# Grouped-query attention: keys written with every head twice, one more weight buffer, scores of two heads between the last query products

## The chip, the cores and the metric

The kernel runs on one core of a Trainium2 chip. The metric is device time of one execution in microseconds (us), the median over runs. The core has TensorE (matrix products; PE in the profile, and PEld for its weight loads), VectorE (DVE), ScalarE (ACT), GpSimd (POOL) and SyncE (SP), which only starts transfers. Each engine works through its own instructions in a fixed order and waits for others by semaphores.

## The reference

One inference step of a two-layer transformer trunk, D = 1024, for 512 latent tokens and 128 context (prompt) tokens. Layer 0 uses neighbourhood attention, layer 1 grouped-query attention with 16 query heads and 4 key heads of width 64. Only layer 1's attention bears on the change:

```python
q, k, v = jnp.split(h @ w_qkv, [1024, 1280], axis=-1)
q = rmsnorm(q.reshape(b, t, 16, 64), q_norm)      # per head
k = rmsnorm(k.reshape(b, t, 4, 64), k_norm)
...
qs = axial_rope(qs); ks_ = axial_rope(ks_)        # latent tokens alone
k_all = jnp.concatenate([ks_, cache_gqa_k[:, i]], axis=1)   # 512 + 128 cached keys
v_all = jnp.concatenate([vs, cache_gqa_v[:, i]], axis=1)
os_ = blocked_attention(qs, k_all, v_all)         # softmax(q k / 8) v, 4 query heads per key head
op = blocked_attention(qp, kp, vp)                # prompt tokens among themselves
```

Behind it come the output product, a residual with adaLN gates, and a gated ConvFFN. The new keys and values of the prompt are outputs too.

## The kernel before

All products run as three passes of split float32 (`hi`, `lo`): each operand is copied to a rounded high part (`wh`, `hT[0]`, `kh`) and a subtraction leaves the low part (`wl`, `hT[1]`, `kl`). The stage of the change lies between layer 0's feed-forward (which ends at about 852 us of the span) and layer 1's output product.

- **Token tiles.** The 640 tokens are five tiles `t` of 128: four latent, and the prompt (`t` = 4). The stage makes 15 product tiles, each a PSUM bank of 128 x 512 by 24 matmuls (`products`, tile name `gp`): first keys and values for `t` = 0 to 4 (`kv_tile`), then the first eight query heads for `t` = 4, 0, 1, 2, 3 (`q_tile`, `hq` = 0), then the other eight for `t` = 0 to 4 (`hq` = 1). Below they are numbered 0 to 14 in that order.
- **Per tile.** `head_rms` squares on ScalarE (`sq`), sums on VectorE (`ssh`), and takes the root on GpSimd (`vh`, `rh`). `head_norm` multiplies by it (`y`) and rotates: cosine product, four sine products into `sq` (VectorE), and their sum on GpSimd (into `kt` or `qt`). The rotation's tables `tab` are made once from `rot` and the gains `gn`, which small transfers on ScalarE's queue bring. Then TensorE transposes the tile into another bank (`turn_k`, `turn_q`, tiles `tk` and `tq`), and copies and subtractions write the high and low parts: `gkh`, `gkl` for keys, each head on both halves of the partitions, `gq` for queries.
- **Weights.** `gqa_w` loads a quarter of a 1024 x 512 group into `wr`, ScalarE copies it into `wh`, VectorE subtracts into `wl`. `wp` has four buffers of each. Those of the next group are split between the products of the last tile of a group (`ahead_of`), as each buffer's last reader is done.
- **Order.** TensorE's order is the order in which the program writes its instructions (`pe`, line 107). `step` holds back the norms by one tile and the transposes by `keep` tiles more, which the list `KP` sets to two for the first four key tiles and one for all others. On the other engines a scheduler orders the instructions by a model of its own.
- **PSUM.** `Banks` (line 74) is a queue: a tile takes the first free bank and is put behind the others when its last reader has been written. `bk.first` prefers one of two pools of four banks (`psx`, `psy`); `bk.drop(4)` takes `psy` out, when it is to be used for scores.
- **Prompt attention** of each key head is three items (`gqa_prompt`: scores, transpose, values) that `PSTEP` deals out behind given query tiles.
- **Units.** Then come 32 units, each a head and half of the latent tokens: scores of two token tiles into a double bank each (`s2`), minimum on VectorE (`nmg`), exponential on ScalarE (`gp`), scaling on GpSimd, transposes (`tp`, `pk`), values (`po`). `GORDER` lists the steps; the scores of a unit are made two units ahead. The scores of units 0 and 1 are written ahead of the first step, behind all query products.

Of the kernel before, what the change touches and what calls it, by code (L numbers as in the profile page):

```python
# [57 lines left out]
PSTEP = (3, 5, 6, 6, 8, 9)  # L58
WU = 29
TP = 1  # L60
PSN = 4
# [4 lines left out]
KP = (2, 2, 2, 2, 1)  # L66
# [35 lines left out]
def hybrid_step(ctx: ExitStack, tc: tile.TileContext, A, O):  # L102
# [1278 lines left out]
    def gqa_w(c0, u, low=None):  # L1381
        return wsplit(rows(wqkv, 2 * u, 2, c0, 512), 2, 512, low)
# [20 lines left out]
    rot = ap.tile([P, 2, 4, HD], F32, name="rot", bufs=1)  # L1403
    nc.scalar.dma_start(rot, A["k_rope"])
# [9 lines left out]
    tab = ap.tile([P, 2, 2, 4, HD], F32, name="tab", bufs=1)  # L1414
    for i in range(2):
        for j in range(2):
            nc.vector.tensor_mul(tab[:, i, j], rot[:, j], gn[:, i, j].unsqueeze(1).broadcast_to([P, 4, HD]))
# [3 lines left out]
    def head_rms(src, n):  # L1421

        sq = ap.tile([P, 8, HD], F32, tag="sq", name="sq")[:, 0:n, :]
        nc.scalar.activation(sq, src, AF.Square)
        ss = sm.tile([P, 8], F32, name="ssh")[:, 0:n]
        nc.vector.tensor_reduce(ss, sq, axis=AX.X, op=ALU.add)
        v = sm.tile([P, 8], F32, name="vh")[:, 0:n]
        nc.gpsimd.tensor_scalar(v, ss, 1.0 / HD, EPS, op0=ALU.mult, op1=ALU.add)
        r = sm.tile([P, 8], F32, name="rh")[:, 0:n]
        last_rms[0] = nc.gpsimd.tensor_tensor(r, v, mhalf.broadcast_to([P, n]), op=ALU.pow)  # L1430
        return sq, r

    def head_norm(dst, src, sq, r, t, i, n):

        y = ap.tile([P, 8, HD], F32, tag="y", name="y")[:, 0:n, :]
        nc.vector.tensor_mul(y, src, r.unsqueeze(2).broadcast_to([P, n, HD]))
        if t == 4:
            nc.vector.tensor_mul(dst, y, gn[:, i, 0].unsqueeze(1).broadcast_to([P, n, HD]))
            return
        nc.vector.tensor_mul(dst, y, tab[:, i, 0, t].unsqueeze(1).broadcast_to([P, n, HD]))  # L1440
# [3 lines left out]
        for b in range(2):  # L1444
            for a in range(2):
                nc.vector.tensor_mul(
                    s5[:, :, a, b, :], y5[:, :, a, 1 - b, :],
                    b4[:, a, b, :].unsqueeze(1).broadcast_to([P, n, 16]),
                )
        nc.gpsimd.tensor_add(dst, dst, sq)  # L1450

    def put_v(c, src):
        nc.scalar.copy(vt[:, c], src.rearrange("p (a d) -> p a d", a=4))

    def turn_k(src, cols):

        tp = bk.get("tk")
        for j in range(2):
            turn(tp[:, j * P : j * P + P], src[:, j * P : j * P + P], ident)
        tv = tp[:, 0:256].rearrange("p (a b) -> p a b", a=2)  # L1460
        for b in range(2):
            own, oth = own_oth(b)
            for part in (own, oth):
                nc.scalar.copy(kh[part, b::2, cols], tv[own])
            for part in (own, oth):
                nc.vector.tensor_sub(kl[part, b::2, cols], tv[own], f32(kh[own, b::2, cols]))
        bk.put(tp)

    def turn_q(src, hq, t):
# [5 lines left out]
        for b in range(2):  # L1475
            own, oth = own_oth(b)
            q = qst[hq][b]
            nc.scalar.copy(q[own, :, cs], tv[own])
            nc.vector.tensor_sub(q[oth, :, cs], tv[own], f32(q[own, :, cs]))
# [18 lines left out]
    def kv_tile(t, ws, *how):  # L1498

        ps = products(t, ws, *how)  # L1500
        st = head_rms(heads(ps[:, 0:256]), 4)
        put_v(t, ps[:, 256:512])
        if t == 4:
            vo = ap.tile([P, 256], F32, tag="kt", name="gvo", bufs=3)
            nc.scalar.copy(vo, ps[:, 256:512])
            nc.scalar.dma_start(O["new_gqa_v"][0, 0].rearrange("t h d -> t (h d)"), vo)

        def norm():
            kt = ap.tile([P, 256], F32, tag="kt", name="kt", bufs=3)
            head_norm(heads(kt), heads(ps[:, 0:256]), *st, t, 1, 4)  # L1510
            if t == 4:
                nc.scalar.dma_start(O["new_gqa_k"][0, 0].rearrange("t h d -> t (h d)"), kt)
            bk.put(ps)
            return lambda: turn_k(kt, slice(t * P, t * P + P) if t < 4 else slice(T, T + P))

        return norm

    def q_tile(t, hq, ws, *how):
        ps = products(t, ws, *how)
        st = head_rms(heads(ps), 8)  # L1520

        def norm():
            if hq and t == 4:
                qt = wp.tile([P, 512], F32, tag="wr", name="qt")
            else:
                qt = ap.tile([P, 512], F32, tag="qt", name="qt", bufs=3)
            head_norm(heads(qt), heads(ps), *st, t, 0, 8)
            bk.put(ps)
            return lambda: turn_q(qt, hq, t)

        return norm
# [29 lines left out]
    ck = ap.tile([P, 256], F32, tag="ck", name="ck", bufs=1)  # L1561
    nc.scalar.dma_start(ck, A["cache_gqa_k"][0, 0].rearrange("t h d -> t (h d)"))
    cv = ap.tile([P, 256], F32, tag="cv", name="cv", bufs=1)
    nc.scalar.dma_start(cv, A["cache_gqa_v"][0, 0].rearrange("t h d -> t (h d)"))
    norms, turns = deque(), deque()

    def step(tile=None, keep=1):
        if tile:
            norms.append(tile)
        while len(norms) > (1 if tile else 0):  # L1570
            turns.append(norms.popleft()())
            if tile:
                break
        while len(turns) > (keep if tile else 1):
            turns.popleft()()

    wqs = [[], []]

    def ahead_of(hq):
        return lambda u: wqs[hq].append(gqa_w(512 * hq, u))  # L1580

    for t in range(NT):
        step(kv_tile(t, wkv, t == 0, ahead_of(0) if t == 4 else None), KP[t])
        if t == 0:
            late[0]()
        elif t == 1:
            late[1]()
            xmp.close()
            pp_s = ExitStack()
            cur = [pp_s.enter_context(pool("prp", 1))]  # L1590
    turns.append(lambda: turn_k(ck, slice(NS, T)))
    put_v(5, cv)
    extra = deque()
    for hq in range(2):
        for n, t in enumerate(((4, 0, 1, 2, 3), (0, 1, 2, 3, 4))[hq]):
            if hq and n == PSN:
                bk.first = psx
            step(q_tile(t, hq, wqs[hq], n == 0, ahead_of(1) if 5 * hq + n == 4 else None))
            i = 5 * hq + n
            if n == 2:  # L1600
                extra.extend(gqa_prompt(2 * hq) + gqa_prompt(2 * hq + 1))
            for _ in range(PSTEP.count(i)):
                extra.popleft()()
    step()
    extra.extendleft(turns)
    pp_s.close()
    hp2.close()
    gqs.close()
    l_o1 = ExitStack()
    op1 = l_o1.enter_context(pool("o1"))  # L1610
    osp1 = [[op1.tile([P, T], F32R, name=f"p{i}{p}") for i in "hl"] for p in range(KC)]
    bk.first = None
    bk.drop(4)
    psy.close()
    with ExitStack() as s:
        ap = s.enter_context(pool("ga", 2, "right"))
        cur = [ap]
        sps = ExitStack()
        sps_p = sps.enter_context(pool("pss", space=PSUM))
        m1 = Mix(1, A["gqa_w_o"][0], lambda p, t: tuple(x[:, t * P : t * P + P] for x in osp1[p]))  # L1620
        ta = {}

        class Unit:


            def __init__(self, u):
                self.b, self.hf, self.p = u % 2, u // 2 % 2, u // 4
                self.h = 2 * self.p + self.b
# [193 lines left out]
```

## Time and profile before

| | us |
|---|---|
| median of three runs (lowest, highest) | 1609.09 (1608.65, 1611.68) |
| the profiled execution | 1610.03 |
| its span in the profile | 1608.2 |
| TensorE busy | 1541.6 (96%) |
| VectorE busy | 1023.0 (64%) |
| ScalarE busy | 860.6 (54%) |
| GpSimd busy | 722.2 (45%) |

The mean granted clock of TensorE was 0.983. A row of the timeline gives the start in us from the span's start, the duration in us, the engine, the line, the operation, what is written `<-` what is read, the shape, how often, and in square brackets the idle time of the engine before it with what ended it. A row of the waits gives who waited for whom: the total in us, how often, the longest. A row of the windows gives a stretch, its length, the busy time and count of PE, PEld, DVE, ACT and POOL, then the granted clock, the share of the transfer engines and GB/s. Line 114 is the helper through which all products go, line 117 that of all transposes, so the tile names tell them apart.

### The profile page before, as it was taken

To read this page: it belongs to the slowest core of one execution; us is meant where nothing else is said; L and a number is where in the kernel's file an instruction comes from. 1 tells how busy PE (TensorE), PEld (TensorE's weight loads), DVE (VectorE), ACT (ScalarE), POOL (GpSimd) and SP (SyncE) were. 2 spreads that over 40 slices of the span, in tenths; PEclk is the share of its full clock that TensorE was granted. 3 is DMA by queue.
4 is the path that set the end of the run, shared out by engine and by line. 5 is a ranking of instruction groups with operands and counts; after the bars stand their busy time and mean duration, and the time that the engine had idled before them with its cause. 6 is when DMAs were issued, how large, how long until landed. Compare 5 with 4: busy or idle time off the path is not lost.

```text
span 1608.2 us, 26065 instructions
## 1 busy us (share of the span) xinstructions
PE 1541.6 (96%) x9709; PEld 1360.4 (85%) x9709; DVE 1023.0 (64%) x1646; ACT 860.6 (54%) x1641; POOL 722.2 (45%) x613
## 2 busy tenths in 40 slices
PE   5999999899999999999999888999999999999998
PEld 3989899777999999988887666778899999998886
DVE  3453533538877666674656867774887888876554
ACT  3474655545565555554453536764555556565343
POOL 1554554324355445544443344441524565553433
PEclk8999999999999999999999998999999999999999
DMA  9745454236456566578573110004634333348664
GB/s 290 185 113 146 117 151 119 62 105 198 144 185 194 199 209 186 193 241 299 170 236 131 60 40 14 2 1 143 211 109 156 105 117 115 104 149 276 206 211 140
DMA packets 193211, 242.42 MB, mean 151 GB/s; under 512 B 11100, under 2 KB 149564, under 8 KB 193084
## 3 DMA queue, kind: packets, MB, share of 16 engines
q1 hardware_dynamic: 182224, 233.13, 45.4%
q10 hardware_dynamic: 10860, 7.62, 2.7%
q8 instruction: 76, 1.25, 0.3%
q14 instruction: 51, 0.42, 0.1%
HBM read 214.38 MB, written 26.34 MB: 150 GB/s over the span
## 4 chain that ended last, share of the span: by engine, by line
PE 73%; DVE 10%; POOL 6%; issue 4%; ACT 4%; DMA 2%; SPq 1%; ACTq 0%; POOLq 0%; DVEq 0%
PE acc L114 18%; PE ux L114 15%; PE y L114 7%; PE uz L114 6%; PE qk L114 5%; PE uy L114 4%; PE po L114 4%; PE s L114 4%; PE vp L114 3%; PE tp L117 3%; PE ada L114 2%; POOL wl L1112 1%; DVE al L1112 1%; POOL vl L1112 1%; DMA wf<-in_ada_w 1%
## 5 line engine op out<-in xcount | busy, mean ns | idle before, releaser
L167 POOL TENSOR_TENSOR wl<-wr,wh 128x1024 fp32r<-128x1024 f32 x74 | 181.5, 2455 | 263.4 <-ACT wh L165 255.2
L1112 POOL TENSOR_TENSOR wl<-wr,wh 128x1024 fp32r<-128x1024 f32 x80 | 194.2, 2448 | 46.1 <-ACT wh L1111 42.6
L114 PE MATMUL ux<-B,wh 128*128 128x322 f32 x832 | 201.9, 314 | 1.4 <-ACT u L1165 0.9
L1188 DVE SCALAR_TENSOR_TENSOR t<-C,cw,t 128x644 f32<-128x644 f32 x176 | 156.3, 888 | 49.1 <-ACT t L1186 48.4
L114 PE MATMUL acc<-wh,alo 128*128 128x512 f32 x440 | 172.3, 392 | 0.6 <-DVE alo L1081 0.6
L114 PE MATMUL acc<-wh,ahi 128*128 128x512 f32 x440 | 171.9, 391 | 0.0
L114 PE MATMUL acc<-wl,ahi 128*128 128x512 f32 x440 | 171.9, 391 | 0.0
L165 ACT CAST wh<-wr 128x1024 fp32r<-128x1024 f32 x140 | 145.5, 1048 | 33.5 <-DMA wr<-in_ffn_w_down 24.3
L114 PE MATMUL uz<-B,wh 128*128 128x322 f32 x640 | 156.5, 313 | 0.7 <-ACT v L1165 0.7
L114 PEld LDWEIGHTS ux<-B,wh 128*128 128x128 f32 x832 | 145.0, 190 | 4.3 <-ACT u L1165 1.2
L1081 DVE TENSOR_TENSOR alo<-ain,ahi 128x384 fp32r<-128x384 f32 (+1 forms) x88 | 77.3, 893 | 89.8 <-ACT ahi L1079 88.8
L114 PE MATMUL ux<-B,wl 128*128 128x322 f32 x416 | 130.1, 313 | 0.2
L114 PE MATMUL qk<-hT,wh 128*128 128x384 f32 (+1 forms) x512 | 122.8, 317 | 0.1
L114 PEld LDWEIGHTS uz<-B,wh 128*128 128x128 f32 x640 | 110.9, 188 | 3.6 <-ACT vh L1111 1.6
L1112 POOL TENSOR_TENSOR vl<-wr,vh 128x1024 fp32r<-128x1024 f32 x38 | 97.1, 2556 | 30.9 <-ACT vh L1111 30.5
L1111 ACT CAST wh<-wr 128x1024 fp32r<-128x1024 f32 x88 | 88.7, 1048 | 32.6 <-DVE wr L1135 31.4
L1186 ACT ACTIVATE t<-C,cw 128x644 f32<-128x644 f32 x88 | 78.6, 893 | 45.9 <-DVE C L1216 43.9
L114 PE MATMUL uz<-B,wl 128*128 128x322 f32 x320 | 99.5, 311 | 0.1
L167 DVE TENSOR_TENSOR wl<-wr,wh 128x1024 fp32r<-128x1024 f32 x66 | 84.5, 1293 | 23.6 <-ACT wh L165 23.1
L114 PEld LDWEIGHTS acc<-wh,alo 128*128 128x128 f32 x440 | 82.5, 188 | 19.1 <-DVE alo L1081 1.4
L1079 ACT CAST ahi<-ain 128x384 fp32r<-128x384 f32 (+1 forms) x88 | 40.1, 460 | 108.4 <-PE acc L114 91.4
L114 PEld LDWEIGHTS acc<-wl,ahi 128*128 128x128 f32 x440 | 82.6, 188 | 17.8
(249 smaller groups left out, 4010.2 us busy)
## 6 DMA issues: line engine op xcount, KB each, us to landing
wr<-in_ffn_w_up SPq DMA_DIRECT2D x88, 512.0 KB
wr<-in_ffn_w_down SPq DMA_DIRECT2D x88, 512.0 KB
wr<-in_ada_w SPq DMA_DIRECT2D x80, 512.0 KB
act<-act SPq DMA_DIRECT2D x44, 321.0 KB
wr<-in_na_w_qkv SPq DMA_DIRECT2D x24, 512.0 KB
mod<-modrow SPq DMA_DIRECT2D x20, 512.0 KB
ain<-act SPq DMA_DIRECT2D x44, 192.0 KB
wf<-in_ada_w SPq DMA_DIRECT2D x16, 512.0 KB
```

The source lines that it names most:

```text
L114: pe(nc.tensor.matmul(*a, **k))
L117: pe(nc.tensor.transpose(*a, **k))
L165: i = nc.scalar.copy(hi, raw)
L167: j = (low or nc.vector).tensor_sub(lo, raw, f32(hi))
L1079: pin(nc.scalar.copy(hi[:, 0 : c1 - c0], ain[:, 0 : c1 - c0]))
L1081: pin(nc.vector.tensor_sub(lo[:, 0 : c1 - c0], ain[:, 0 : c1 - c0], f32(hi[:, 0 : c1 - c0])))
L1111: nc.scalar.copy(hl[0], src)
L1112: low.tensor_sub(hl[1], src, f32(hl[0]))
L1186: nc.scalar.activation(t, taps(0), AF.Identity, bias=cw[:, 3, n : n + 1], scale=cw[:, 1, n : n + 1])
L1188: nc.vector.scalar_tensor_tensor(t, taps(d), cw[:, w, n : n + 1], t, op0=ALU.mult, op1=ALU.add)
```

## The change

- Keys are normed into a tile that holds every head twice, side by side (`kd`): the last addition writes both, or for the prompt two multiplications do. `turn_k` then makes four transposes instead of two and one copy and one subtraction over 128 partitions instead of four and four over 64. The cached keys are loaded twice into the same shape; the cached values go straight into `vt`.
- A pool `wx` holds one more `wh` and `wl`. Of each group one weight is split some tiles ahead, two during the last tile of the group before, and one behind it; two of the four subtractions go to GpSimd.
- `Prep` takes the place of `kv_tile`, `q_tile` and `step`. Of each tile the square sums are written within the next tile's products, its transposes behind the products two tiles on and ahead of the norm of the tile between. The table `KP` is gone.
- `bk.first` prefers `psx` from tile 10 on (before: tile 14), and `psy` is dropped at tile 12, where the scores' pool takes its place. The scores of units 0 and 1 are written within the products of tiles 12, 13 and 14 (`ESC`: tile and quarter, unit and half); their probabilities lie in four `wr` buffers. The last query tile is turned ahead of unit 2's step.
- `PSTEP` (now counted over all 15 tiles) puts the prompt's items behind tiles 8, 9, 10, 10, 11, 12; before it was, in that count, 8, 10, 11, 11, 13, 14.
- `pk` has five buffers of 512 instead of six. `rot` is gone: the table is loaded into `tab` and multiplied there. `o` returns its argument.

```diff
-PSTEP = (3, 5, 6, 6, 8, 9)
+PSTEP = (8, 9, 10, 10, 11, 12)
+ESC = {(12, 2): (0, 0), (13, 1): (0, 1), (13, 3): (1, 0), (14, 2): (1, 1)}
-PSN = 4
-KP = (2, 2, 2, 2, 1)
...
+    wx = gqs.enter_context(pool("wx", 1, "right"))
+    tab = ap.tile([P, 2, 2, 4, HD], F32, name="tab", bufs=1)
+    nc.scalar.dma_start(tab[:, 1], A["k_rope"])
...
+        if twice is not None:
+            dst, sq = (x.unsqueeze(2).broadcast_to([P, n, 2, HD]) for x in (dst, sq))
+        o(nc.gpsimd.tensor_add(dst if twice is None else twice, dst, sq))
...
     def turn_k(src, cols):
 
         tp = bk.get("tk")
-        for j in range(2):
-            turn(tp[:, j * P : j * P + P], src[:, j * P : j * P + P], ident)
-        tv = tp[:, 0:256].rearrange("p (a b) -> p a b", a=2)
-        for b in range(2):
-            own, oth = own_oth(b)
-            for part in (own, oth):
-                nc.scalar.copy(kh[part, b::2, cols], tv[own])
-            for part in (own, oth):
-                nc.vector.tensor_sub(kl[part, b::2, cols], tv[own], f32(kh[own, b::2, cols]))
+        for g in range(4):
+            turn(tp[:, g * P : g * P + P], src[:, g].rearrange("p a b -> p (a b)"), ident)
+        tv = tp.rearrange("p (a b) -> p a b", a=4)
+        o(nc.scalar.copy(kh[:, :, cols], tv))
+        o(nc.vector.tensor_sub(kl[:, :, cols], tv, f32(kh[:, :, cols])))
         bk.put(tp)
...
+    ck = ap.tile([P, 4, 2, HD], F32, name="ck", bufs=1)
+    for b in range(2):
+        nc.scalar.dma_start(ck[:, :, b, :], A["cache_gqa_k"][0, 0])
+    nc.scalar.dma_start(vt[:, 5], A["cache_gqa_v"][0, 0])
...
+    tiles = [Prep(None, t) for t in range(NT)]
+    tiles += [Prep(hq, t) for hq in range(2) for t in ((4, 0, 1, 2, 3), (0, 1, 2, 3, 4))[hq]]
+    group = [wkv, [], []]
+    extra = deque()
+    for i, x in enumerate(tiles):
+        g = i // NT
+
+        def after(u):
+            if u == 0:
+                if i:
+                    tiles[i - 1].stat()
+            if i % NT == 4 and g < 2:
+                if u < 2:
+                    group[g + 1].append(gqa_w(512 * g, u + 1, (None, nc.gpsimd)[u], wx if g and u == 0 else None, False))
+            if (i, u) in ESC:
+                v, j = ESC[i, u]
+                if v not in un:
+                    un[v] = Unit(v)
+                un[v].scores(j)
+
+        if i == 10:
+            bk.first = psx
+        if i == 12:
+            bk.drop(4)
+            psy.close()
+            sps_p.append(sps.enter_context(pool("pss", space=PSUM)))
+        x.products(group[g], i % NT == 0, after)
+        if i > 1:
+            tiles[i - 2].turns()
+        if i == 2:
+            turn_k(ck, slice(NS, T))
+        if i:
+            tiles[i - 1].norm()
+        if i % NT == 4 and g < 2:
+            group[g + 1].append(gqa_w(512 * g, 3, None, None, False))
+        if i == 0:
             late[0]()
...
+            group[1].append(gqa_w(0, 0, nc.gpsimd, wx, False))
+        elif i == 6:
+            group[2].append(gqa_w(512, 0, nc.gpsimd, None, False))
+        elif i == 7:
+            extra.extend(gqa_prompt(0) + gqa_prompt(1))
+        for _ in range(PSTEP.count(i)):
+            extra.popleft()()
+    bk.first = None
+    extra.extend(gqa_prompt(2) + gqa_prompt(3))
+    tiles[-1].stat()
+    tiles[-2].turns()
+    tiles[-1].norm()
...
         for u in range(NU + 2):
+            if u == 2:
+                tiles[-1].turns()
```

294 lines of the change are left out of this document (134 added, 160 removed).

## The prediction

> **What bounds the kernel now.** I read the page first (busy shares, chain), then TensorE's waits in the layer-1 query/key stage (852 to 982 us, the only stretch that the edit rewrites), then each engine's timeline there, and the granted clock by the microsecond.
>
> ```profile
> PE 1541.6 (96%) x9709; PEld 1360.4 (85%) x9709; DVE 1023.0 (64%) x1646; ACT 860.6 (54%) x1641; POOL 722.2 (45%) x613
> PE 73%; DVE 10%; POOL 6%; issue 4%; ACT 4%; DMA 2%; SPq 1%; ACTq 0%; POOLq 0%; DVEq 0%
> ```
> ```profile
> PE s L114 <- ACT gp L1648: 6.4, 2, 5.6
> PE gp L114 <- ACT wh L165: 3.6, 2, 1.9
> PE tq L117 <- POOL qt L1450: 2.8, 2, 2.0
> PE tk L117 <- POOL kt L1450: 2.5, 2, 1.8
> PE gp L114 <- DVE wl L167: 1.2, 3, 0.4
> PE tp L117 <- DVE gq L1479: 1.1, 1, 1.1
> ```
> ```profile
> 887.49 3.10 PE L114 MATMUL gp<-wh,hT 128*128 128x512 f32 x12 [1.71 <-ACT wh L165]
> 894.48 0.44 PE L117 MATMUL tk<-ident,kt 128*128 128x128 f32 x2 [1.77 <-POOL kt L1450]
> 921.70 4.04 PE L114 MATMUL gp<-wh,hT 128*128 128x512 f32 x16 [1.88 <-ACT wh L165]
> 937.40 0.91 PE L117 MATMUL tq<-ident,qt 128*128 128x128 f32 x4 [2.03 <-POOL qt L1450]
> 970.16 0.90 PE L114 MATMUL s<-gkh,gq 128*128 128x320 f32 x2 [5.62 <-ACT gp L1648]
> ```
> ```profile
> 937.00:938.00 1.00, 0.60 (x4) 0.51 (x4) 0.97 (x2) 0.60 (x1) 0.35 (x1) 0.83 0.00 0
> 944.00:945.00 1.00, 1.00 (x4) 0.77 (x4) 0.94 (x3) 0.63 (x4) 0.00 (x0) 0.76 0.00 0
> 968.00:969.00 1.00, 0.00 (x0) 0.00 (x0) 0.97 (x2) 0.00 (x0) 0.77 (x2) 0.69 0.00 0
> 978.00:979.00 1.00, 1.00 (x8) 0.96 (x7) 0.26 (x1) 0.95 (x3) 0.80 (x1) 0.69 0.75 291
> ```
>
> TensorE bounds the kernel at 96%. All its waits in the stage come to 6.4 + 3.6 + 2.8 + 2.5 + 1.2 + 1.1 = 17.6 us, and two of them are followed by half clock (third column from the end): from 937.8 to 944.75 after the 2.03 us wait, from 968.7 to 978.7 after the 5.62 us one. At half rate that costs 6.9 / 2 = 3.4 us, and 3.9 us (970.16 to 978.7 without a wait of 0.8, halved). So 17.6 + 7.3 = 25 us is all that the edit can win; TensorE's own work in it stays.
>
> **Part by part.** First the three places that it relieves.
>
> *First query tile*, waits of 1.71 and 1.77 us: four weight splits queue behind the key copies of a packed stage. A key tile now takes one copy and one subtraction instead of four and four, and the first weight is split ahead into the new buffer. I give back all: **-3.5**.
>
> ```profile
> L167 POOL TENSOR_TENSOR wl<-wr,wh 128x1024 fp32r<-128x1024 f32 x74 | 181.5, 2455 | 263.4 <-ACT wh L165 255.2
> ```
> ```profile
> 892.62 3.50 DVE L1466 TENSOR_TENSOR gkl<-tk,gkh 64x256 fp32r<-64x256 f32 x8
> 921.68 6.48 DVE L167 TENSOR_TENSOR wl<-wr,wh 128x1024 fp32r<-128x1024 f32 x4 [0.19 <-ACT wh L165]
> ```
>
> *Second weight change*, 1.88 plus two of 0.4: one weight is ready early and VectorE has two of the four subtractions. The exponentials that hold up ScalarE here stay, so I leave 1.0: **-1.7** (ends -2.7 and 0). The two subtractions that move to GpSimd take 2.46 each there; one runs long before its use, the other beside TensorE's first 16 products of the tile (4.04), and GpSimd's norms queued behind it have a tile of slack. *The third wait*, 2.03, is the echo of those 6.48 us; it goes with its half clock: **-5.4** (ends -5.4, 0).
>
> *End of the products*: waits of 0.8, 5.62, 0.8 and 1.1 and the 3.9 us, 12.2 in all. Four scores now run between products, so exponentials are ready when the units begin. Late next: the turn of tile 13, whose rotation ends some 8 us after its products (3.6 to its norm in the bank rows below, then steps of 0.69, 0.69, 0.9 and 1.29 and a subtraction between), about 1.4, the bank of tile 12's turn (1.7), the exponential of unit 2 (0.8), some 0.6 more, and 2 of half clock: 6.5 stay, **-5.7** (ends -10 and 0).
>
> Now what it adds. *Transposes*: a key tile has four instead of two, six tiles, 0.09 us each (four take 0.35 in the bank rows below): **+1.1**.
>
> *The first key turn comes a tile earlier.* Before, the turns lag three tiles for the first keys; now two. The turn of tile 0 stands on TensorE right behind the products of tile 2.
>
> ```profile
> 859.00 0.68 DVE L368 TENSOR_TENSOR xm<-acc,mod 128x512 f32<-128x512 f32 x1
> 860.92 1.29 DVE L387 TENSOR_TENSOR xm<-xo,mod 128x512 f32<-128x512 f32 x2
> 862.23 0.34 ACTq L1404 DMA_DIRECT2D rot<-in_k_rope  x1
> 866.33 0.48 PE L114 MATMUL gp<-wh,hT 128*128 128x512 f32 x1
> 874.94 0.42 DVE L1417 TENSOR_TENSOR tab<-rot,gn 128x256 f32<-128x256 f32 x1 [1.67 <-DMA gn<-in_gqa_k_norm]
> 877.63 0.72 POOL L1450 TENSOR_TENSOR kt<-kt,sq 128x256 f32<-128x256 f32 x1 [0.55 <-DVE sq L1446]
> 878.41 0.44 PE L117 MATMUL tk<-ident,kt 128*128 128x128 f32 x2 [0.72 <-POOL kt L1450]
> 908.26 1.29 POOL L1450 TENSOR_TENSOR qt<-qt,sq 128x512 f32<-128x512 f32 x1 [3.28 <-DVE sq L1446]
> ```
>
> Those products end at 866.33 + 5.6 = 871.9. The rotated key starts its last step only at 877.63, because the table waits for the norm's load until 874.94, and that step, written twice, has the query's width: 1.29 instead of 0.72. Ready at 878.9: a wait of 7.1. The tables move in memory: the old one lies where the modulation read until 862.2 was, the new one where that read until 859.7 was, so the loads can start up to 2.5 earlier; then 4.5. I take 5.5, less the 0.72 that is there already, plus 3.4 of half clock: **+8.2** (ends 2.8 without half clock, 9.8). Queued behind it: the cached keys' turn and all later products.
>
> *Fewer accumulator banks in the last five query tiles.* This is the largest term. From tile 10 on banks are taken from four (`psx`) while these are free, and from tile 12 there are only four. I followed the queue of free banks by hand, from the order in which layer 0 leaves it. The first prompt scores behind tile 10's products take the bank that the turn of tile 8 has just filled, with only the prompt's values between. Tile 12's products take that of tile 9's turn, with only a prompt turn between; tile 13's that of tile 10's, with the prompt's values between. TensorE works in the written order, so it stands until that bank is copied out. How long this takes:
>
> ```profile
> 948.27 0.60 PE L117 MATMUL tq<-ident,qt 128*128 128x128 f32 x4
> 948.62 0.48 PE L114 MATMUL gp<-wh,hT 128*128 128x512 f32 x1
> 949.02 0.57 ACT L1478 CAST gq<-tq 64x512 fp32r<-64x512 f32 x1
> 949.88 0.68 DVE L1479 TENSOR_TENSOR gq<-tq,gq 64x512 fp32r<-64x512 f32 x1
> 950.60 0.58 ACT L1478 CAST gq<-tq 64x512 fp32r<-64x512 f32 x1 [1.00 <-DVE gq L1479]
> 951.89 0.69 DVE L1436 TENSOR_TENSOR y<-gp,rh 128x512 f32<-128x512 f32 x1 [1.33 <-POOL rh L1430]
> 952.61 0.69 DVE L1479 TENSOR_TENSOR gq<-tq,gq 64x512 fp32r<-64x512 f32 x1
> 954.28 0.60 PE L117 MATMUL tq<-ident,qt 128*128 128x128 f32 x4
> 954.71 0.60 PE L117 MATMUL tp<-ident,pp 128*128 128x128 f32 x4
> 974.66 1.06 PE L117 MATMUL tq<-ident,qt 128*128 128x128 f32 x4
> 979.60 0.69 DVE L1479 TENSOR_TENSOR gq<-tq,gq 64x512 fp32r<-64x512 f32 x1
> 980.43 0.63 PE L117 MATMUL tp<-ident,gp 128*128 128x128 f32 x4 [1.05 <-DVE gq L1479]
> ```
>
> A query turn is copied out in four steps, each waiting for the one before: copy 0.57, subtraction 0.68, copy 0.58, subtraction 0.69. The last starts after the norm of a younger tile, which itself waits for GpSimd, and ends at 953.30, 4.7 us after TensorE was free at 948.62. That such a wait is real the last row shows: the one bank used again so soon (turned at 974.66, free at 980.29) held TensorE for 1.05 us. The edit does not change these steps. With 0.4 of other work between, each wait is 4.3 us: 12.9. Each is over twice the 2.03 us that was followed by half clock: 3 x 3.4 = 10.2. **+23.1** (ends: 2.4 each and no half clock, 7.2; 6 each, 28.5).
>
> On SP's queue the weight loads keep their order; the output weights' loads now wait for the four raw buffers that units 0 and 1 hold, and are wanted only behind the units: nothing. Five `pk` buffers in place of six cost nothing, since the values that read the oldest stand on TensorE ahead of the next turn. The cached values' copy goes, and the cached keys load twice: both far from a wait, or behind the first key's.
>
> Sum: -3.5 - 1.7 - 5.4 - 5.7 + 1.1 + 8.2 + 23.1 = +16.1. The profiled execution took 1610.03 us (span 1608.2), 0.9 above the median of the three runs, 1609.09; so 1625.2 in the median.
>
> **The clock, weighed against the Trainium skill.** The rows give half clock for 6.9 us after a restart without further waits. The Trainium skill, TensorE: Matmul & The Clock Gate, section "Part 1: The HAM clock gate", has full clock come back after one busy window of some 3.4 us. By the row a throttling costs 3.4 us; by that rule half, and the sum would be 1618. The trace disagrees with it, having two such lengths. The section also asks for an idle window of some 3.4 us before it throttles; the 2.03 us wait, which no such window fits into, speaks against that.
>
> **Rivals.** *A, half clock lasts half as long*: 1.7 less at each of four places, 6.8: 1618. The 6.9 us speak against it; that waits sit apart by a tile for it. *B, the copying out is short*: turns are now written ahead of the norms, so the second subtraction may go ahead of the norm. The bare chain is 3.1 us, the waits 2.7, and 1.71, 1.77 and 1.88 us were followed by no half clock: 23.1 becomes 8.1, and the time 1610. In the quoted turn the norm went first although the copy was done 0.7 us earlier. *C, faster: the three banks are not waited for*, because the pool gives others than I follow: 23.1 less, 1602. It decides once the three waits cost under 4 us together. For it: only one such wait is in the old trace. Against it: that one, and the queue as written. *D, the waits spread*: the first units turn into the same four banks, each copied 4.7 us after its turn, and two more waits come at the end: 1633.
>
> **The numbers.** Forecast 0.45 (1625; its own range 1612 to 1637), A 0.15, B 0.12, C 0.16, D 0.12. The runs shown lie within 0.2% (3.2 us), which is what can be told from no change. Slower by more: forecast, A and D, 0.72; within: B, 0.12; faster: C, 0.16. The range 1602 to 1637 leaves out half of C and some of D.
>
> **What would show it.** TensorE's waits of the changed kernel: a key turn behind tile 2 waiting 4 to 7 us for GpSimd or the norm's load; prompt scores, and the products of tiles 12 and 13, each waiting about 4 us for the last query subtraction; half clock behind each; no wait for `wh` at the first query tile; and no 5.62 us wait ahead of the second unit's scores. Wrong it would be if waits for `gq` are missing or under 2 us, or if the first key's load lands by 870.

## The result, and the profile after

The changed kernel took 1634.38 us in the median of four runs (1630.55 to 1635.12), beside 1609.53 (1608.65 to 1611.68) of the kernel before on the same chip: a ratio of 1.0144, 95% interval 1.0130 to 1.0159, 24.9 us slower. The profiled execution took 1634.21 us, its span 1632.4, with a mean granted clock of 0.975.

In the page of the changed kernel TensorE still bounds; it is busy 4.7 us longer, and its share of the longer span is one point lower:

```profile
PE 1546.3 (95%) x9721; PEld 1367.2 (84%) x9721; DVE 1014.5 (62%) x1625; ACT 854.0 (52%) x1622; POOL 739.5 (45%) x617
```

Where the time went is seen from two instructions that both kernels have: the first product of the stage and the first value product of the units. Below, first the kernel before, then the changed one: the row of the timeline at which the stage starts, and the group of the value products, with the start of the first and the end of the last.

```profile
852.69 3.88 PE L114 MATMUL gp<-wh,hT 128*128 128x512 f32 x16
L114 PE MATMUL po<-pk,gvt x320: 379/379/431, 982.8 to 1115.9; 128*64 128x256 f32 x160
```
```profile
852.23 3.87 PE L113 MATMUL gp<-wh,hT 128*128 128x512 f32 x16
L113 PE MATMUL po<-pk,gvt x320: 378/379/431, 1007.0 to 1140.2; 128*64 128x256 f32 x160
```

From the one to the other the kernel before took 982.8 - 852.69 = 130.1 us, the changed one 154.8. The value products take 133.1 and 133.2, and what follows them 492.3 and 492.2. So all of the 24.7 us lies in the rewritten stage. This length, "the stage", is used below for every kernel.

TensorE's waits in the stage (total, how often, longest), and the rows of the timeline of the long ones:

```profile
PE tk L116 <- POOL kd L1459: 12.9, 1, 12.9
PE gp L113 <- DVE gq L1484: 8.3, 2, 4.2
PE sp L113 <- DVE gq L1484: 4.0, 1, 4.0
PE tp L116 <- POOL pp L643: 3.6, 1, 3.6
PE tp L116 <- DVE gq L1484: 3.3, 1, 3.3
PE s L113 <- ACT gp L1608: 2.0, 1, 2.0
PE gp L113 <- DVE wl L166: 0.4, 1, 0.4
PE tq L116 <- POOL qt L1459: 0.4, 1, 0.4
```
```profile
884.55 1.11 PE L116 MATMUL tk<-ident,kd 128*128 128x128 f32 x4 [12.89 <-POOL kd L1459]
934.21 1.11 PE L116 MATMUL tp<-ident,pp 128*128 128x128 f32 x4 [3.62 <-POOL pp L643]
948.13 0.44 PE L113 MATMUL sp<-gkh,gq 128*128 128x128 f32 x1 [3.99 <-DVE gq L1484]
962.45 0.76 PE L113 MATMUL gp<-wh,hT 128*128 128x512 f32 x1 [4.14 <-DVE gq L1484]
976.30 0.76 PE L113 MATMUL gp<-wh,hT 128*128 128x512 f32 x1 [4.18 <-DVE gq L1484]
```

They come to 34.9 us, before to 17.6. The first prompt scores (`sp`) and two tiles' products (`gp`) wait for the last subtraction of a query turn, that is for its bank. Two other long ones are those for the prompt's probabilities `pp`, which before appear in no wait of the stage, and for the first key `kd`, the longest of all (before, `kt`: 0.72 for the first key, 1.77 for a later one).

The granted clock (third column from the end): at the two ends of the half clock around the first bank wait, then over the stretches around the waits of 3.6, 4.0, 4.2, the last two, and the key's:

```profile
946.00:947.00 1.00, 0.00 (x0) 0.00 (x0) 0.44 (x1) 0.00 (x0) 0.53 (x1) 0.96 0.00 0
953.00:954.00 1.00, 1.00 (x4) 0.81 (x3) 0.00 (x0) 0.00 (x0) 0.00 (x0) 0.62 0.00 0
930.00:945.00 15.00, 10.52 (x41) 8.00 (x39) 10.43 (x18) 6.36 (x11) 10.00 (x8) 0.77 0.00 0
945.00:955.00 10.00, 6.87 (x23) 5.84 (x24) 4.15 (x11) 2.09 (x9) 3.85 (x3) 0.66 0.01 2
970.00:985.00 15.00, 10.82 (x44) 8.38 (x42) 5.97 (x13) 3.60 (x9) 4.70 (x5) 0.77 0.00 0
995.00:1005.00 10.00, 4.97 (x21) 4.56 (x22) 6.63 (x12) 4.67 (x11) 6.98 (x11) 0.66 0.04 2
875.00:890.00 15.00, 5.45 (x19) 4.70 (x20) 7.13 (x24) 1.82 (x4) 4.98 (x8) 0.54 0.12 37
```

The bank wait runs from 944.14 to 948.13. Half clock starts at 946.9, 2.8 us into it, and ends at 953.8: 10 x 0.34 x 2 = 6.8 us, of which 5.6 fall behind the wait and cost 2.8. The other stretches, and that around the wait of 4.1 (960.6 to 967.4), have 6.8 or 6.9 us too, placed so that 3.0 are lost behind the wait of 3.6, 2.5 and 2.4 behind the other two bank waits, and 2.4 at the end. The key wait has 15 x 0.46 x 2 = 13.8 us of half clock (13.7 by rows of 1 us), from 875 on, but most of it passes while TensorE stands; the 4.3 us between 884.55 and 888.8 cost 2.1.

### The profile page after: what moved, and what is told of

It is laid out like the page before. It is cut to its first block, busy times and chain, and to the rows that moved or that the text cites. A ratio compares the mean times of both kernels' runs of the same rounds, so it can differ in the third digit from the quotient of the medians.

```text
span 1632.4 us, 26032 instructions
## 1 busy us (share of the span) xinstructions
PE 1546.3 (95%) x9721; PEld 1367.2 (84%) x9721; DVE 1014.5 (62%) x1625; ACT 854.0 (52%) x1622; POOL 739.5 (45%) x617
## 4 chain that ended last, share of the span: by engine, by line
PE 75%; DVE 9%; POOL 5%; issue 4%; ACT 3%; DMA 2%; SPq 1%; ACTq 0%; POOLq 0%; DVEq 0%
PE acc L113 18%; PE ux L113 15%; PE y L113 7%; PE uz L113 6%; PE qk L113 5%; PE uy L113 4%; PE po L113 4%; PE gp L113 4%; PE s L113 3%; PE vp L113 3%; PE tp L116 3%; PE ada L113 2%; POOL wl L1111 1%; DVE t L1187 1%; DVE al L1111 1%
## 5 line engine op out<-in xcount | busy, mean ns | idle before, releaser
L166 POOL TENSOR_TENSOR wl<-wr,wh 128x1024 fp32r<-128x1024 f32 x78 | 193.4, 2481 | 266.8 <-ACT wh L164 248.0
L1111 POOL TENSOR_TENSOR wl<-wr,wh 128x1024 fp32r<-128x1024 f32 x80 | 194.2, 2448 | 46.0 <-ACT wh L1110 42.3
L113 PE MATMUL ux<-B,wl 128*128 128x322 f32 x416 | 129.5, 311 | 0.2
L113 PEld LDWEIGHTS acc<-wh,ahi 128*128 128x128 f32 x440 | 82.6, 188 | 17.7
```

What stands on the lines that cost most here:

```text
L113: pe(nc.tensor.matmul(*a, **k))
L166: j = (low or nc.vector).tensor_sub(lo, raw, f32(hi))
L1111: low.tensor_sub(hl[1], src, f32(hl[0]))
```

## The experiments

Theory: each wait read above costs its length and the half clock behind it. Rivals: the key turn alone costs; or the slack is refilled, so that other engines hold TensorE up wherever one wait is removed. All times are medians; the kernel before stood at 1609.3 to 1610.2 beside them.

**The bank waits, removed in two ways.** The first writes the scores of units 0 and 1 late again, so that eight banks are there to the end:

```diff
-ESC = {(12, 2): (0, 0), (13, 1): (0, 1), (13, 3): (1, 0), (14, 2): (1, 1)}
+ESC = {}
-        if i == 10:
+        if i == 14:
             bk.first = psx
-        if i == 12: (drop psy, open the scores' pool)
+    (both behind the loop, then the scores of units 0 and 1)
```

> The scores of units 0 and 1 are written behind all query products again, and the prompt's and the query tiles' banks come from all eight until then; all else stays as in the changed kernel. Theory (each wait read in the changed kernel costs its length and a stretch of half clock behind it): the three waits for a query turn's bank, 3.99 + 4.14 + 4.18 = 12.3 us, go, with some 3.4 us of half clock behind each, 10.2; about 6 us come back at the end of the products, where the exponentials of units 0 and 1 are late again. 1634.4 - 12.3 - 10.2 + 6 = about 1618; the key turn's wait of 12.9 us stays. Rival 'the key turn alone': the bank waits only take the place of others, so at most 5 us are won: 1629 or more. Rival 'the slack is refilled' (VectorE, ScalarE and GpSimd are late there whatever TensorE does): waits for gq go and others of like length appear, 1630 or more.

It took 1619.74 us, 14.6 less (ratio to before 1.0060, 1.0043 to 1.0078), the stage 136.5. No products or prompt scores wait for `gq`; 3.0 us of such a wait are at the units' first scores. The second keeps the early scores and changes the order:

```diff
-        if i == 10:
+        if i == 11:
             bk.first = psx
         x.products(group[g], i % NT == 0, after)
+        if i:
+            tiles[i - 1].norm()
         if i > 1:
             tiles[i - 2].turns()
         ...
-        if i:
-            tiles[i - 1].norm()
```

> The scores of units 0 and 1 stay between the query products. Two changes of order: the norm of a tile is written ahead of the turn of the tile before it, and the four banks are preferred from tile 11 on instead of tile 10. Followed by hand, no product and no prompt score then takes a bank that has just been turned into. Theory: the three bank waits go (12.3 us and about 10 of half clock), the key turn's 12.9 stays, perhaps longer by a little since its norm is no earlier: about 1612. Rival 'the scores themselves cost' (their minima and exponentials crowd out the norms, whatever the banks): the waits for gq go but waits for qt or kd of like length take their place, 1628 or more. If the first kernel with late scores is faster than this one by over 5 us, the scores between the products cost something besides the banks.

It took 1616.91 us, 17.5 less (1.0040, 1.0026 to 1.0055), the stage 137.3. TensorE's waits in it, then VectorE's rows ahead of the new longest one:

```profile
PE tk L116 <- POOL kd L1459: 13.0, 1, 13.0
PE s L113 <- ACT gp L1608: 5.9, 1, 5.9
PE tp L116 <- POOL pp L643: 3.6, 1, 3.6
PE tq L116 <- POOL qt L1459: 2.0, 1, 2.0
```
```profile
983.37 0.69 DVE L1442 TENSOR_TENSOR qt<-y,gn 128x512 f32<-128x512 f32 x1
984.09 1.56 DVE L1607 TENSOR_REDUCE nmg<-s 128x1 f32<-128x640 f32 x2
```

Every wait for `gq` is gone; a norm (`qt`) takes 1.6 us more in their place. So 14.6 and 17.5 us hang on the banks, which neither rival, the key turn alone or refilled slack, would give. The rows also suggest why early scores win little: unit 3's scores need the buffer of unit 2's, whose minimum (`nmg`) stands on VectorE behind the last tile's norm (983.37). The wait of 5.6 us at the end has moved by one pair of units and is 5.9. The two kernels do not differ by 5 us in favour of late scores (by the medians the early ones are 2.8 better, by the stage 0.8 worse), so the scores show no cost besides the banks either.

**The key turn a tile later.**

```diff
-        if i > 1:
-            tiles[i - 2].turns()
-        if i == 2:
+        for j in {1: (), 2: (), 3: (0,), 4: (1, 2)}.get(i, (i - 2,)) if i else ():
+            tiles[j].turns()
+        if i == 5:
             turn_k(ck, slice(NS, T))
```

> The first keys' turns lag three tiles again: tile 0 behind the products of tile 3, tiles 1 and 2 behind tile 4, tile 3 and the cached keys behind tile 5; all else stays. Theory: the 12.9 us wait for the first rotated key goes, and with it the half clock of 875 to 890 us (about 4 us): 1634.4 - 12.9 - 4 = about 1618, or up to 3 more if the third tile's turns come while the copies of the weights stand in front of them. Rival 'banks alone': nothing behind the key turn depends on its time and the wait comes back at the third weight change, 1630 or more.

1632.87 us (1.0143, 1.0128 to 1.0158), 1.5 less, which is within the spread of the changed kernel's runs; the stage 151.5, 3.3 less. Theory and expectation failed: though the turn is due 5.6 us later, TensorE still waits 8.0 for `kd`, and 3.1 for GpSimd's weight subtraction. Nor are the 3.3 us won at the key. The bank waits are as long as in the changed kernel, but behind two of them, and behind the wait for `pp`, half clock lasts only 3.4 us here, some 3 us less loss in all. The first of the two, to be held against the 0.66 of the same stretch above (10 x 0.17 x 2 = 3.4):

```profile
945.00:955.00 10.00, 8.19 (x33) 6.79 (x34) 3.81 (x10) 1.51 (x8) 2.53 (x3) 0.83 0.01 2
```

The same delay on top of the mended banks:

> Both: norms ahead of turns with the four banks from tile 11, and the first keys' turns three tiles behind. Theory: the two gains add, 22 and 17 us, 1634.4 - 39 = about 1596, faster than before the change. If the waits are refilled by one another the sum is smaller: 1609 to 1612 is what the kernel before would give.

1616.25 us (1.0040, 1.0027 to 1.0053), the stage 134.4; the gains do not add. So the key is late wherever its turn stands, later than the 878.9 that the prediction worked out from the old rows. What makes it late is read in the changed kernel. First ScalarE and its queue, then SyncE's queue, VectorE and GpSimd:

```profile
864.27 1.05 ACT L164 CAST wh<-wr 128x1024 fp32r<-128x1024 f32 x1 [2.44 <-DVE xm L392]
864.27 0.35 ACTq L1404 DMA_DIRECT2D tab<-in_k_rope  x1
866.15 0.48 ACTq L1407 DMA_DIRECT2D gn<-in_gqa_k_norm  x1
867.67 4.24 ACTq L1575 DMA_DIRECT2D ck<-in_cache_gqa_k  x2
867.81 0.37 SPq L162 DMA_DIRECT2D wr<-in_gqa_w_qkv  x1
871.97 0.38 ACT L1426 ACTIVATE sq<-gp 128x256 f32<-128x256 f32 x1 [6.65 <-DMA gn<-in_gqa_k_norm]
879.03 0.42 DVE L1416 TENSOR_TENSOR tab<-tab,gn 128x256 f32<-128x256 f32 x1 [4.82 <-DMA gn<-in_gqa_k_norm]
883.23 1.26 POOL L1459 TENSOR_TENSOR kd<-kt,sq 128x512 f32<-128x512 f32 x1 [2.06 <-DVE sq L1453]
```

Three things stand in these rows. The copy into the new buffer waits until 864.2 for memory that the modulation still reads, and the table's and norms' loads stand behind it on ScalarE, 2.0 us later than the 862.23 of before. Issuing the doubled cached keys holds ScalarE 4.24 us, so the square sum comes at 871.97. And as soon as the early split has released its raw buffer, the next weight load starts, at 867.81, beside the norm's load, which lands 12.9 us after its issue.

**The cached keys' loads later** (issued behind the second tile, turned behind tile 3):

```diff
-    for b in range(2):
-        nc.scalar.dma_start(ck[:, :, b, :], A["cache_gqa_k"][0, 0])
-    nc.scalar.dma_start(vt[:, 5], A["cache_gqa_v"][0, 0])
...
         elif i == 1:
             ...
+            (the same three loads)
```

> The loads of the cached keys and values are issued after the second token tile instead of ahead of all, and the cached keys are turned one tile later; all else as in the changed kernel. Theory (the key turn waits because the norm's load, issued just ahead of the doubled cached keys on ScalarE's queue, lands at 879.0 instead of 874.9, and because issuing those two loads holds ScalarE for 4.24 us): the load lands 3 to 4 us earlier, the key wait of 12.9 falls to about 9, and 1634.4 becomes about 1630. Rival 'the late issue' (the loads start 2 us later, behind the copy into the new weight buffer, and that is all): the wait stays at 12 or more, 1634. Rival 'nothing but the turn's place': 12.9 stays.

1632.81 us (1.0146, 1.0131 to 1.0161), the stage 151.7. The square sum comes at 867.96 and the key wait falls to 10.2, but the norm's load still lands only at 879.36, where VectorE's wait for it ends, and the loads of `ck` start at 868.06, just behind the square sum, and hold ScalarE for 7.1 us: the edit took them out of the way of the first square sum, not out of the norm's. That the wait falls by 2.7 us comes from VectorE's order. The addition of the squares, in the changed kernel and in this one:

```profile
879.37 0.41 DVE L1428 TENSOR_REDUCE ssh<-sq 128x4 f32<-128x256 f32 x1
873.29 0.41 DVE L1428 TENSOR_REDUCE ssh<-sq 128x4 f32<-128x256 f32 x1
```

In the changed kernel the squares were there at 872.4 and VectorE stood idle from 874.2 to 879.0, but the addition was placed behind the table's last product, which waits for the load; the key's last step began 4.2 us after the start of that product. Here the scheduler placed the addition ahead of it, and the step began 1.4 us after. So the holding of ScalarE by itself does not set the first key in the changed kernel, and what delays the load is open here.

**The split into the new buffer later** (behind tile 3 instead of 1, kept in that place of the order):

```diff
         elif i == 1:
             ...
-            group[1].append(gqa_w(0, 0, nc.gpsimd, wx, False))
+        elif i == 3:
+            group[1].append(gqa_w(0, 0, nc.gpsimd, wx, True))
```

> The weight that is split ahead into the new buffer is split behind the fourth token tile instead of the second; all else as in the changed kernel. ScalarE's queue then holds no copy that waits for the modulation's memory ahead of the table's load, so the loads may start at about 862.2 as before, 2.0 earlier. If the late issue is what delays the key: the wait of 12.9 falls by 2, to 11. The first query tile waits again for its weights, about 1 to 3.5 us as before, so the time stays at 1632 to 1636. If the wait falls by far more than 2 the copy blocked more than the issue.

1629.62 us, 4.8 less (1.0127, 1.0110 to 1.0144), the stage 148.1. The rows that answer to those above:

```profile
862.49 0.35 ACTq L1404 DMA_DIRECT2D tab<-in_k_rope  x1
865.26 0.58 ACTq L1407 DMA_DIRECT2D gn<-in_gqa_k_norm  x1
874.47 0.42 DVE L1416 TENSOR_TENSOR tab<-tab,gn 128x256 f32<-128x256 f32 x1 [1.48 <-DMA gn<-in_gqa_k_norm]
879.99 1.11 PE L116 MATMUL tk<-ident,kd 128*128 128x128 f32 x4 [6.54 <-POOL kd L1459]
```

The wait halves, by 6.4 and not by 2, and no wait for weights comes instead, though that for `pp` grows from 3.6 to 4.5. Counted from the start of the stage (854.02 here), the norm's load was issued 2.7 us earlier than in the changed kernel and took 3.7 less, which makes the 6.4. The load took 9.2 us from issue to the table, not 12.9, although the cached keys' loads follow it just as closely; what no longer runs beside it is the weight load. To test that, this kernel got a weight load of its own at that time:

```diff
         if i == 0:
+            nc.sync.dma_start(wx.tile([P, 2, 512], F32, tag="wl", name="spare"), rows(wqkv, 0, 2, 0, 512))
```

> The kernel with the new buffer's split late, plus a load of 512 KB of weights on SyncE's queue into the new buffer's second half, which nothing reads: it runs at the time of the norms' loads, as the weight load at 867.81 did in the changed kernel. If a weight transfer beside it is what makes the key's norm land late: it lands 2 to 4 us later than the 874.5 of the kernel without it, and the key wait grows from 6.5 to 9 or 10. If only the issue time counted: the landing stays within 0.5 of 874.5 and the wait at 6.5.

```profile
863.59 0.55 ACTq L1407 DMA_DIRECT2D gn<-in_gqa_k_norm  x1
864.92 0.37 SPq L1689 DMA_DIRECT2D spare<-in_gqa_w_qkv  x1
875.06 0.43 DVE L1416 TENSOR_TENSOR tab<-tab,gn 128x256 f32<-128x256 f32 x1 [2.69 <-DMA gn<-in_gqa_k_norm]
876.60 0.42 DVE L1428 TENSOR_REDUCE ssh<-sq 128x4 f32<-128x256 f32 x1 [1.11 <-ACT sq L1426]
881.79 1.12 PE L116 MATMUL tk<-ident,kd 128*128 128x128 f32 x4 [9.47 <-POOL kd L1459]
```

1632.49 us (1.0139, 1.0123 to 1.0154), the stage 151.9. In absolute time the load lands 0.6 later, less than expected, but it was issued 1.7 earlier: 11.5 us instead of 9.2, and the wait is 9.5, as expected. (The stage began at 852.89 here, 1.1 earlier; counted from there the landing is 1.7 later.) Part of the wait is not the load: the issue of the cached keys began only at 874.81, for a reason that the trace does not show, and the square sum came behind it (1.11 us of wait ahead of `ssh`). So beside a weight transfer the load took 2.3 us more, of the 3.7 by which it took longer in the changed kernel; the other 1.4 stay unexplained. The test is not clean, since the cached keys' loads no longer ran beside the norm's. But the other traces divide in the same way: from issue to use, the last of the norms' loads took 11.9 to 13.5 us in seven kernels in which the weight load starts beside it, and 8.8 to 10.6 in the five without, the kernel before among them. Issuing the cached keys held ScalarE 3.7 us or more wherever that weight load ran, but 1.3 in the four kernels with the split late and no load added. How the weight load slows the other is not shown: from 868 to 870 the mean share of the transfer engines was 0.05 in the changed kernel, so they were not full. The Trainium skill, DMA: Bandwidth & Descriptors, section "Queues, rings and completion order", has each transfer engine take turns between its queues, packet by packet. The 11.5 us against 9.2 do not contradict that, but no run here shows the turns.

**Can the change be made to win?** The banks mended, the cached keys late, and the key's norm loaded ahead of the query's:

```diff
-    for i, nm in enumerate(("gqa_q_norm", "gqa_k_norm")):
+    for i, nm in ((1, "gqa_k_norm"), (0, "gqa_q_norm")):
...
-    for i in range(2):
+    for i in (1, 0):
```

> The order that avoids the banks just turned (norms ahead of turns, the four banks preferred from tile 11), with the cached keys' loads late as above, and the key's norm loaded, and its table made, ahead of the query's. The key's load then lands about where the query's does in the changed kernel, some 5 us earlier than 879. Theory: key wait of 12.9 down to 3 to 5, little half clock behind it: 1616.9 - 9 - 2 = about 1606. If the square sums or GpSimd and not the load set the key, the wait stays above 8 and the time at 1612 or more.

1615.89 us (1.0039, 1.0025 to 1.0052), the stage 133.9. The table of the key was ready at 873.4, yet the wait is 10.0. VectorE works in order, and the query's gain, whose load now lands last, stood ahead of the key's norm:

```profile
878.13 0.23 DVE L1415 TENSOR_SCALAR gn<-gn 128x128 f32<-128x128 f32 x1 [3.86 <-DMA gn<-in_gqa_q_norm]
878.28 0.42 DVE L1439 TENSOR_TENSOR y<-gp,rh 128x256 f32<-128x256 f32 x1
```

The prompt's steps back in their old places, on top of it (`PSTEP` 8, 10, 11, 11, 13, 14; the four banks preferred from tile 12):

```diff
-PSTEP = (8, 9, 10, 10, 11, 12)
+PSTEP = (8, 10, 11, 11, 13, 14)
-        if i == 11:
+        if i == 12:
             bk.first = psx
```

> The kernel above with the prompt's steps behind tiles 8, 10, 11, 11, 13, 14, as before the change, and the four banks preferred from tile 12 on. The wait of 3.6 us for the prompt's probabilities and the half clock behind it (about 3 us) go: some 6 us less than the kernel above, about 1600. If the scores of unit 0 now wait for the last readers of the four other banks, up to 3 of it come back.

1613.82 us (1.0025, 1.0016 to 1.0035), the stage 133.3. The wait for `pp` went, but 3.2 us came for the prompt scores' bank ahead of a unit's scores and 3.3 for `gq` at the end: 2 us of the 6. Then all of it, written against the kernel before this one, with the split late, the first key's turn behind tile 3, and the prompt's steps in places whose banks are free:

```diff
-PSTEP = (8, 9, 10, 10, 11, 12)
+PSTEP = (8, 10, 10, 11, 12, 13)
-        if i > 1:
-            tiles[i - 2].turns()
+        for j in ({1: (), 2: (), 3: (0, 1)}.get(i, (i - 2,)) if i else ()):
+            tiles[j].turns()
-        if i == 3:
+        if i == 4:
             turn_k(ck, slice(NS, T))
-            group[1].append(gqa_w(0, 0, nc.gpsimd, wx, False))
+        elif i == 3:
+            group[1].append(gqa_w(0, 0, nc.gpsimd, wx, True))
-            extra.extend(gqa_prompt(0) + gqa_prompt(1))
+            a, b = gqa_prompt(0), gqa_prompt(1)
+            extra.extend((a[0], a[1], b[0], a[2], b[1], b[2]))
```

> Norms ahead of turns and the four banks from tile 11; the key's norm loaded ahead of the query's; the new buffer's split behind the fourth token tile; the cached keys' loads late, their turn behind tile 4; the first key's turn behind tile 3 (the second's with it, the rest two tiles behind as in the changed kernel); the prompt's steps behind tiles 8, 10, 10, 11, 12, 13 with the second head's scores ahead of the first one's values. Theory: of the kernel with the banks mended (1616.9) the key wait of 13 and its half clock of about 4, and the probabilities' wait of 3.6 with 3 of half clock, go; the 5.9 us wait at the end stays: 1616.9 - 17 - 6 = about 1594, below the 1609 of before. Rival 'slack refilled': where one wait goes the next engine is late, as in the two kernels that mended one thing each and won 1.5: 1608 or more.

```profile
PE s L113 <- ACT gp L1606: 4.3, 1, 4.3
PE tk L116 <- POOL kd L1460: 3.8, 1, 3.8
PE tq L116 <- DVE gq L1485: 2.5, 3, 1.2
PE gp L113 <- POOL wl L166: 2.2, 1, 2.2
PE tq L116 <- POOL qt L1460: 1.6, 1, 1.6
```

1608.42 us in eleven runs, ratio 0.9991 (0.9983 to 1.0000); the stage 127.0, 3.1 less than before. It is 26 us better than the changed kernel, but not told apart from the one before: the stage began 2.1 us later in this trace, and over all traces that start lies between 850.3 and 855.2, though no experiment edits what precedes it. The waits, 14.8 us with one of 0.4 for weights, stand a little under the 17.6 of before: the expected 1594 took the refilling too lightly. The same with late scores (as in the first experiment, and the last two prompt steps behind tiles 13 and 14):

```diff
-ESC = {(12, 2): (0, 0), (13, 1): (0, 1), (13, 3): (1, 0), (14, 2): (1, 1)}
+ESC = {}
-PSTEP = (8, 10, 10, 11, 12, 13)
+PSTEP = (8, 10, 10, 11, 13, 14)
```

> The kernel above with the scores of units 0 and 1 behind all query products again, so that all eight banks are there to the end. If scores between the products are worth the 6 us that the prediction put on them (by shorter waits at the end), this kernel is some 6 us slower than the one above; if they win nothing (the two kernels that mended the banks in the one and the other way stood at 1616.9 and 1619.7), it is within 3.

1610.34 us (1.0002, 0.9993 to 1.0011), the stage 128.6. With the prompt steps that moved along, the early scores are worth about 1.9 us (1.6 by the stage) once their banks are paid, not 6. And the kernel with all mended, early scores included, with the first keys three tiles behind:

```diff
-        for j in ({1: (), 2: (), 3: (0, 1)}.get(i, (i - 2,)) if i else ()):
+        for j in ({1: (), 2: (), 3: (0,), 4: (1, 2)}.get(i, (i - 2,)) if i else ()):
-        if i == 4:
+        if i == 5:
             turn_k(ck, slice(NS, T))
```

> The kernel with all mended, and the first keys three tiles behind instead: tile 0 behind the products of tile 3, tiles 1 and 2 behind tile 4, tile 3 and the cached keys behind tile 5. There the third key was ready at 883.9 and held TensorE for 3.8 us, with half clock behind it. Theory: that wait goes and with it 1.7 of half clock, 1608.4 - 5.5 = about 1603, under the kernel before by 0.4%. Rival: GpSimd's weight subtraction, awaited 2.2 us at the second weight change, is then awaited longer by most of it, and the time stays at 1607 to 1608.

1609.10 us (0.9994, 0.9985 to 1.0003), the stage 129.5. The key wait fell to 0.6 and the rival won: GpSimd's weight subtractions are now awaited 5.7 us in two waits, the longer 3.7, and VectorE's part of the weights 1.3. The weights are now late by what the keys were. No version beats the kernel before by more than the measurement can tell.

## Why the prediction was right, and where it was off

The forecast of slower held, and 1634.4 lies within the range of 1602 to 1637, 9 above the 1625. By its own terms (measured: the wait in the trace plus the half clock that falls behind it):

| term | predicted | in the trace |
|---|---|---|
| first query tile | -3.5 | -3.5 (no wait left) |
| second weight change | -1.7 | -2.7 (no wait left) |
| third wait, with its half clock | -5.4 | +1.2 (3.6 + 3.0 - 5.4) |
| end of the products | -5.7 | -4.1 (8.1 - 12.2) |
| transposes | +1.1 | not measured alone |
| first key turn | +8.2 | +14.3 (12.9 - 0.7 + 2.1) |
| three banks | +23.1 | +20.0 (12.3 + 7.7) |

With 1.1 for the transposes that is 26.3, against 24.7 in the stage. The total came out better than its terms: the key turn and the third wait each cost over 6 us more than forecast and lie outside their stated ends (2.8 to 9.8, -5.4 to 0), while banks and second weight change came out 4 us lower. That the time is inside the range is owed to the range's width.

Some readings of the old trace were off, without changing the forecast. A row of 1 us with 0.83 holds 0.34 us of half clock, not 0.17, so half clock ran from 937.7 to 944.5 and from 968.4 to 978.6: one stretch of 6.8 us and one of 10.2. Two ends do not follow from their terms: for the key 4.5 less 0.7 is 3.8 and not 2.8, for the banks three times 6 and 10.2 is 28.2 and not 28.5.

*The banks* were right in mechanism and place: 3.99, 4.14 and 4.18 us where 4.3 each was forecast. The half clock was over-sized, 2.4 to 2.8 behind each instead of 3.4, since it begins within the wait. The two kernels that removed the waits won 14.6 and 17.5 us. Rivals B (short copies) and C (no bank wait) fell. Rival A had a smaller loss per wait, but in the changed kernel for another reason, since half clock does last 6.8 us there. Its 3.4 us do occur, though, behind two of the same bank waits in the kernel with the key turn a tile later: the length is not fixed by the wait, so the 6.9 forecast behind each was partly luck. D's time, 1633, was the nearest, but only a part of its mechanism came: one of its two further bank waits, the 3.3 us at the end.

*The first key turn* was the most mis-sized of the added costs. "The loads can start up to 2.5 earlier" was wrong: they started 2.0 later, because on ScalarE's queue the new buffer's copy stands ahead of them. The wait of 12.9 us is the 7.1 that was worked out ahead of that credit and three things more, each counted from the start of the stage and against the kernel before. The norm's load was issued 2.2 us later (864.38 before, 866.15 after). It took 12.9 us instead of 10.6, which is 2.3 more; the weight load that the split releases runs beside it. From the table to the key's last step it is 4.2 us instead of 2.7, which is 1.5 more, since VectorE added the squares (`ssh`) only behind the table, at 879.37; before, it did so at 872.86, ahead of the table's last product at 874.94. (The products ended 0.2 later than reckoned.) The doubled cached keys' loads were put at nothing ("far from a wait"); their 4.24 us on ScalarE show no cost by themselves there. Without the early split the wait was 6.5, near the 7.1, in part by chance: the load took 1.4 us less than before the change, and VectorE's order cost 1.5.

*The third wait* was said to go. The wait for `qt` went, but the prompt's steps were moved and priced only by their banks, not by their own chain:

```profile
924.27 0.27 PE L113 MATMUL sp<-gkl,gq 128*128 128x128 f32 x1
932.13 2.03 POOL L643 TENSOR_TENSOR pp<-pp,rcp 128x512 f32<-128x512 f32 x1
```

From the last score at 924.5 to the scaled probabilities at 934.2 are 9.6 us, and the transposes now come one tile (5.6 us of products) later instead of two.

*The end* kept more than thought: 3.3 for a bank, 2.0 for an exponential, 0.4, and 2.4 of half clock, 8.1 where 6.5 was forecast. The kernels with early and late scores show that the early ones win little there, since the next pair of units waits instead.

## What to carry to other kernels

Fewer accumulator banks are paid where a bank just filled is taken again, and then by the whole length of its copying out: list the order of the free banks before trading them for anything. Work moved ahead must be looked up in its engine's queue: what does it wait for, what waits behind it, and which transfer starts when it releases its buffer? Look also where a finished input stands in the next engine's order. Removing one wait does not always win its length: the banks gave back 14.6 and 17.5 us of their 20, but the later key turn 1.5 of an expected 17 and the later prompt steps 2 of 6, as other engines were late instead. In all 26 us were recovered, which is the old time again and hardly more.

## What was not expected of the hardware

In the changed kernel half clock lasted 6.8 to 6.9 us after each of four waits of 3.6 to 4.2 us, beginning 2.8 us into the bank wait shown, and 13.7 us around a wait of 12.9, of which 4.3 fell behind it; so the longest wait cost no more clock behind it (2.1 us) than the short ones (2.4 to 3.0). The lengths are not the waits' own: in the stage of all fourteen traces half clock lasts 3.4, 6.8, 10.2 or 13.7 us, and its starts within a trace lie whole multiples of 3.41 us apart (13.64, 13.66, 13.66 and 23.88 between the last five of the changed kernel). Bank waits of 4.0 and 4.15 us that were followed by 6.8 us there were followed by 3.4 in the kernel with the key turn a tile later.

A load of a norm took 9.2 us without and 11.5 with a 512 KB weight load beside it. Issuing two loads of the cached keys held ScalarE between 1.32 us (the kernel with the split late), 4.24 (the changed one) and 7.1 (the one with these loads later).
